# Seven half-size products in place of eight in a feed-forward down projection, its weight sums made in DRAM

## The chip, the cores and the metric

The kernel runs on one core of a Trainium2 chip. The metric is the device time of one execution in microseconds (us), lower being better. Every time below comes from one profiled execution or from the three timed runs of the kernel before.

## The reference, cut to what matters

The network has 512 tokens of width 1024 in float32. A first block (two attention-like mixers and a feed-forward block) is followed by four attention layers. The change lies in the feed-forward block of the first block:

```
h = rmsnorm(x, norm_ffn)
x = x + (silu(h @ w_ffn_gate) * (h @ w_ffn_up)) @ w_ffn_down
x = rmsnorm(x, norm_final)
```

`w_ffn_gate` and `w_ffn_up` are 1024 x 2816, `w_ffn_down` is 2816 x 1024. The hidden width 2816 is 22 chunks of 128.

## The kernel before

Matrix products are float32 products made of three terms: each operand is split into a high part (float32r, made by a copy on ScalarE, L214) and a low part (what is left, made by a subtraction on VectorE, L215), and TensorE adds high x high, low x high and high x low (`mm3`, L270 to L277). `split_into` (L213) is that pair of operations. Weights come by DMA on SyncE's queue (SP) into `wraw`, which has three buffers of 128 x 1024, and their splits go to `wpool`, which has six buffers each for high and low. `X` holds the residual, tokens by width; `Ah` and `Al` hold the normalized activations, width by tokens, already split.

`mixer1` (L425) is the first block's attention part. In `nsa` (L717) a small network compresses keys and values; its small weights `w2t` are the last DMAs (L744) that GpSimd (POOL) issues before the attention's scores. POOL's next work is the broadcast of a gain (`gf`, L858) and, block by block of 128 tokens, the two small operations of `rms_scale` (L377): a multiply-add and a power. `merge` (L850) ends the mixer; its `epilogue` (L873) adds a product to X, sums squares, calls `rms_scale`, scales, and `to_feat` (L361) transposes the block on TensorE into `Ah` and `Al`.

`ffn` (L963) works on the hidden width in three parts of 8, 8 and 6 chunks (`FF_PARTS`, L33). The first four chunks take whole gate and up products (L981 to L993) while `half_sums` (L886) makes sums of halves of the activations. All later chunks go two at a time through `pair` (L999): the gate products of two neighbouring chunks are made as seven products of half size by `halves_product` (L909), from sums of quarters of the two chunks' weights and of the activations; the two up products are whole; then come the silu, the product with up (`hidden`, L975) and the split into `hdh` and `hdl`. After the chunks of a part, `down` (L1026) multiplies them by their rows of `w_ffn_down` through `out_proj` (L397): for each half of 512 output columns and each block of 128 tokens one product over the part's chunks into a PSUM bank, then an update of X (L1029):

```
nc.vector.scalar_tensor_tensor(out=xv, in0=ps, scalar=0.5, in1=xv, op0=ALU.mult, op1=ALU.add)
```

In the last part, squares (L1033), the norm with `gf` (L1038) and `to_feat` (L1039) follow block by block, and the first products of the next layer (`mla`, L1107) read `Ah` and `Al`.

The order of instructions on each engine is worked out when the kernel is built, by a scheduler with a timing model that goes by program order where two instructions could both run; `after` (L341) adds an order by hand. Each engine then works strictly in that order. A DMA that needs another one's result waits on the engine that issues it.

Of the kernel before, what the change touches and what calls it, by code (L numbers as in the profile page):

```python
# [18 lines left out]
S = 512  # L19
# [13 lines left out]
FF_PARTS = (8, 8, 6)  # L33
# [94 lines left out]
class Net:  # L128
    def __init__(self, ctx, tc, a):
# [6 lines left out]
        self.small = pool("small", 4)  # L136
        ps = lambda name, bufs: ctx.enter_context(tc.tile_pool(name=name, bufs=bufs, space=PSUM))
# [579 lines left out]
    def nsa(self, w, gate, kp, vv, qu, spare, rope, fill_gate, fill_up, fill_last):  # L717
        nc, a, tc = self.nc, self.a, self.tc
        with ExitStack() as c1:
# [8 lines left out]
            for i, (pe, w1, w2) in enumerate((("cmp_pe_k", "cmp_k_w1", "cmp_k_w2"), ("cmp_pe_v", "cmp_v_w1", "cmp_v_w2"))):  # L728
# [14 lines left out]
                for r in range(2):  # L743
                    nc.gpsimd.dma_start(w2t[:, r], a[w2][0])  # L744
# [140 lines left out]

    def half_sums(self, pool, room):  # L886

# [3 lines left out]
        f11, f21, f12, f22 = (room.tile([128, 4, 256], F32, name=n) for n in ("f11", "f21", "f12", "f22"))  # L891
        for f, k, tok in ((f11, lo, t0), (f22, hi, t1), (f21, lo, t1), (f12, hi, t0)):
            nc.vector.tensor_tensor(out=f, in0=q(self.Ah, k, tok).bitcast(F32), in1=q(self.Al, k, tok).bitcast(F32), op=ALU.add)
        nc.vector.tensor_tensor(out=f22, in0=f21, in1=f22, op=ALU.add)
        nc.vector.tensor_tensor(out=f21, in0=f11, in1=f21, op=ALU.subtract)
        nc.vector.tensor_tensor(out=f11, in0=f22, in1=f11, op=ALU.subtract)
        nc.vector.tensor_tensor(out=f12, in0=f12, in1=f11, op=ALU.subtract)
        out = {"a11": (q(self.Ah, lo, t0), q(self.Al, lo, t0)), "a12": (q(self.Ah, hi, t0), q(self.Al, hi, t0)), "a22": (q(self.Ah, hi, t1), q(self.Al, hi, t1))}

        def splits():  # L900
            for n, src in (("s2", f11), ("s3", f21), ("s1", f22), ("s4", f12)):
                h, l = (pool.tile([128, 4, 256], F32R, name=n + u) for u in "hl")
                self.split_into(h, l, src)
                out[n] = (h, l)
            return out

        return splits

    def halves_product(self, pool, raws, sums, w, n0, out):  # L909
# [5 lines left out]
        v1 = self.wload(w, 0, KD, (n0 + 128, 128), pool=raws)  # L915
# [16 lines left out]
        def product(ps, wt, k0, name, first=False, last=False):  # L932
            sh, sl = sums[name]
            for k in range(4):
                (ah, al), (bh, bl) = (wt[0][:, k0 + k], wt[1][:, k0 + k]), (sh[:, k], sl[:, k])
                for i, (x, y) in enumerate(((ah, bh), (ah, bl), (al, bh))):
                    nc.tensor.matmul(ps, lhsT=x, rhs=y, start=first and k == 0 and i == 0, stop=last and k == 3 and i == 2, skip_group_check=True)  # L937
# [21 lines left out]
        product(a, w3, 4, "a22", last=True)  # L959
        out(0, 1, a, None)  # L960
        yield

    def ffn(self):  # L963
        nc, a, tc = self.nc, self.a, self.tc
        with ExitStack() as c1:
            f1 = c1.enter_context(tc.tile_pool(name="f1", bufs=1))
            raws = c1.enter_context(tc.tile_pool(name="fr", bufs=1))
            most = max(FF_PARTS)
            hd = [f1.tile([128, most, S], F32R, name=n) for n in ("hdh", "hdl")]
            st = f1.tile([128, NB, 2], F32, name="fss")  # L970
            gf = f1.tile([128, D], F32, name="gf")
            self.broadcast_row(gf, a["norm_final"])
            wg, wu = a["w_ffn_gate"][0], a["w_ffn_up"][0]

            def hidden(m, s, u, tok=slice(0, S)):  # L975
                nc.vector.tensor_tensor(out=s, in0=s, in1=u, op=ALU.mult)
                self.split_into(hd[0][:, m, tok], hd[1][:, m, tok], s)


            with tc.tile_pool(name="f0", bufs=1) as f0:  # L980
                for m in (0, 2):  # L981
                    wgs, wus = self.w_cols(wg, m * 128), self.w_cols(wu, m * 128)
                    for t in range(2):
                        halves = 1 if m or t else 2
                        for hf in range(halves):
# [5 lines left out]
                            s = f0.tile([128, S], F32, name="fg", bufs=2)[:, 0:n]  # L991
                            self.silu2(s, pg)
                            hidden(m + t, s, pu, tok)  # L993
# [482 lines left out]
```

## Time and profile before

| what | value |
|---|---|
| three timed runs | 1867.27, 1861.35, 1867.57 us |
| median | 1867.27 us |
| profiled execution, its own time | 1861.58 us |
| profiled execution, span from first to last instruction | 1859.8 us |
| mean granted TensorE clock | 0.998 |

The span and its parts below belong to the one profiled execution. PE is TensorE's matmuls, PEld its weight loads (which overlap matmuls), DVE is VectorE, ACT ScalarE, POOL GpSimd, SP SyncE; L12 is line 12 of the kernel. A group of instructions reads "line engine operation output<-inputs, shape, xcount | busy time, mean ns of one | idle time of the engine just before". The granted clock is a share of 2.4 GHz.

### The profile page before, as it was taken

What the parts mean: (1) busy time and instruction counts of PE and PEld (TensorE: products, weight loads), DVE (VectorE), ACT (ScalarE), POOL (GpSimd) and SP (SyncE); (2) the same over time, 40 slices, a digit from 0 to 9 for tenths busy, and PEclk for the clock granted to TensorE, in tenths of its full rate; (3) what the DMA queues carried; (4) which work ended last, traced back from release to release, by engine and by line L of the source; (5) the groups of instructions that cost most, each with busy time, mean ns of one, the idle gap of its engine ahead of it and who ended that gap; (6) DMA issues with size and microseconds to landing.
All of it is one profiled execution on the core that took longest, in us unless ns stands there. A gap on an engine that the chain in (4) does not pass through costs nothing.

```text
span 1859.8 us, 27095 instructions
## 1 busy us (share of the span) xinstructions
PE 1815.6 (98%) x10023; PEld 1492.6 (80%) x10023; DVE 1215.3 (65%) x3050; ACT 905.9 (49%) x2024; POOL 153.9 (8%) x213
## 2 busy tenths in 40 slices
PE   7999999999999999999999999999999999999997
PEld 7877787678888988889887798777888877988775
DVE  5554387754854664656878675576776666788866
ACT  4543236743432442435666434573565563366651
POOL 2211100000000000001000011341000000200001
PEclk9999999999999999999999999999999999999999
DMA  7222141042332342333121233211432222232111
GB/s 219 79 59 57 36 128 41 19 146 79 103 96 74 112 127 79 91 94 98 54 69 58 64 91 98 68 56 39 115 78 60 78 80 69 76 88 59 48 56 46
DMA packets 200751, 148.13 MB, mean 80 GB/s; under 512 B 8765, under 2 KB 178538, under 8 KB 200618
## 3 DMA queue, kind: packets, MB, share of 16 engines
q1 hardware_dynamic: 198826, 140.97, 26.4%
q0 software_dynamic: 1792, 5.42, 0.9%
q8 instruction: 79, 1.29, 0.3%
q14 instruction: 54, 0.44, 0.1%
HBM read 144.27 MB, written 2.10 MB: 79 GB/s over the span
## 4 chain that ended last, share of the span: by engine, by line
PE 91%; DVE 4%; ACT 2%; issue 2%; DMA 1%; POOL 0%; SPq 0%; POOLq 0%; DVEq 0%; ACTq 0%
PE pj L273 22%; PE pj L275 22%; PE pj L276 21%; PE o L350 4%; PE t L337 3%; PE pj L937 3%; PE s L937 1%; PE o L273 1%; PE o L276 1%; PE o L275 1%; PE s L275 1%; PE s L273 1%; PE s L276 1%; PE s L311 1%; DVE wl L215 1%
## 5 line engine op out<-in xcount | busy, mean ns | idle before, releaser
L214 ACT ACTIVATE wh<-wr 128x1024 fp32r<-128x1024 f32 (+9 forms) x406 | 294.6, 755 | 402.7 <-PE pj L275 162.5
L215 DVE TENSOR_TENSOR wl<-wr,wh 128x1024 fp32r<-128x1024 f32 (+9 forms) x406 | 337.8, 855 | 217.6 <-ACT wh L214 212.8
L273 PE MATMUL pj<-Ah,wh 128*128 128x512 f32 (+1 forms) x888 | 348.0, 392 | 2.2 <-DVE fg L288 0.9
L275 PE MATMUL pj<-Al,wh 128*128 128x512 f32 (+1 forms) x888 | 347.3, 391 | 0.2 <-DVE Al L215 0.2
L276 PE MATMUL pj<-Ah,wl 128*128 128x512 f32 (+1 forms) x888 | 346.0, 390 | 0.0
L273 PE MATMUL pj<-wh,Ah 128*128 128x512 f32 (+5 forms) x640 | 218.9, 343 | 4.4 <-ACT Ah L214 4.2
L275 PE MATMUL pj<-wl,Ah 128*128 128x512 f32 (+5 forms) x640 | 216.5, 338 | 0.0
L276 PE MATMUL pj<-wh,Al 128*128 128x512 f32 (+5 forms) x640 | 214.7, 339 | 0.9 <-DVE Al L215 0.9
L273 PEld LDWEIGHTS pj<-Ah,wh 128*128 128x128 f32 x888 | 168.1, 189 | 37.1 <-PE s L276 1.6
L276 PEld LDWEIGHTS pj<-Ah,wl 128*128 128x128 f32 x888 | 168.0, 189 | 34.7 <-issue 1.5
L275 PEld LDWEIGHTS pj<-Al,wh 128*128 128x128 f32 x888 | 168.0, 189 | 33.3 <-issue 0.8
L327 ACT ACTIVATE sp<-sp,nm 128x128 f32<-128x128 f32 (+3 forms) x256 | 142.9, 559 | 75.5 <-DVE nm L326 73.4
L205 ACT ACTIVATE pt<-t 128x512 f32<-128x512 f32 (+3 forms) x288 | 115.4, 445 | 103.7 <-PE t L337 66.7
L324 DVE CUSTOM_DVE_ANT_0 sp<-s,c_causal 128x128 f32<-128x128 f32 (+3 forms) x256 | 121.0, 486 | 56.6 <-PE s L276 23.5
L273 PEld LDWEIGHTS pj<-wh,Ah 128*128 128x128 f32 x640 | 121.3, 190 | 19.4 <-ACT Ah L214 7.0
L276 PEld LDWEIGHTS pj<-wh,Al 128*128 128x128 f32 x640 | 121.0, 189 | 12.8 <-DVE Al L215 2.0
L275 PEld LDWEIGHTS pj<-wl,Ah 128*128 128x128 f32 x640 | 121.4, 190 | 10.8 <-issue 0.2
L337 PE MATMUL t<-ident,sp 128*128 128x128 f32 x640 | 108.9, 278 | 5.1 <-ACT pt L205 4.8
L337 PEld LDWEIGHTS t<-ident,sp 128*128 128x128 f32 x640 | 77.3, 140 | 30.8 <-ACT pt L205 12.8
L331 DVE TENSOR_SCALAR sp<-sp,rc 128x128 f32<-128x128 f32 (+3 forms) x256 | 96.7, 383 | 5.0
L273 PE MATMUL pj<-wh,hdh 128*128 128x512 f32 x176 | 68.5, 390 | 0.3 <-DVE X L1029 0.3
L275 PE MATMUL pj<-wl,hdh 128*128 128x512 f32 x176 | 68.7, 390 | 0.0
(478 smaller groups left out, 3344.9 us busy)
## 6 DMA issues: line engine op xcount, KB each, us to landing
wr<-in_w_in_dram SPq DMA_DIRECT2D x34, 512.0 KB, 3.8
wr<-in_fox_w_in_dram SPq DMA_DIRECT2D x30, 512.0 KB, 4.1
wr<-in_w_ffn_gate_dram SPq DMA_DIRECT2D x22, 512.0 KB, 3.9
wr<-in_w_ffn_up_dram SPq DMA_DIRECT2D x22, 512.0 KB
wr<-in_w_ffn_down_dram SPq DMA_DIRECT2D x22, 512.0 KB, 3.9
wr<-in_swa_w_in_dram SPq DMA_DIRECT2D x20, 512.0 KB, 3.8
wr<-in_mla_w_in_dram SPq DMA_DIRECT2D x16, 512.0 KB, 4.0
wr<-in_mla_w_out_dram SPq DMA_DIRECT2D x16, 512.0 KB, 3.8
```

Of the source, the lines that this page charges most:

```text
L205: return self.nc.scalar.activation(out, in_, AF.Copy, scale=1.0 if scale is None else scale)
L214: self.nc.scalar.activation(h, src, AF.Copy)
L215: self.nc.vector.tensor_tensor(out=l, in0=src, in1=h.bitcast(F32), op=ALU.subtract)
L273: mm = self.nc.tensor.matmul(ps, lhsT=ah, rhs=bh, start=i == 0, stop=False)
L275: self.nc.tensor.matmul(ps, lhsT=ah, rhs=bl, start=False, stop=False)
L276: mm = self.nc.tensor.matmul(ps, lhsT=al, rhs=bh, start=False, stop=i == n - 1)
L324: nc.vector.tensor_tensor_reduce(out=v, in0=ps, in1=self.causal[:, S - n:S], scale=1.0, scalar=LOWEST, op0=ALU.add, op1=ALU.max, accum_out ...
L327: nc.scalar.activation(v, v, AF.Exp, bias=nm[:, g], accum_out=sm[:, g])
L331: nc.vector.tensor_scalar(v, v, rc[:, g], None, ALU.mult)
L337: nc.tensor.transpose(ps[:, (b - j) * 128:(b - j + 1) * 128], sp[:, POFF[b] + j * 128:POFF[b] + j * 128 + 128], self.ident)
L350: mm = self.nc.tensor.matmul(po[64 * i:64 * i + 64, j * 128:S], lhsT=value(j, i), rhs=pt[:, TOFF[j]:TOFF[j] + (NB - j) * 128], start=first ...
L937: nc.tensor.matmul(ps, lhsT=x, rhs=y, start=first and k == 0 and i == 0, stop=last and k == 3 and i == 2, skip_group_check=True)
```

## The change

`w_ffn_down` is taken as 2 x 2 quarters of 1408 x 512: b11, b12, b21, b22. The hidden activations are taken as 2 x 2 as well (two halves of tokens, and even against odd chunk of a pair, where a pair is now chunk c and chunk c + 11). The down product then takes seven products of half size. Four of them use sums of weight quarters, t1 = b11 + b12, t3 = b22 + b12, t2 = b22 + t1, t4 = b21 + t2, and three use b11, b22 and b21. The sums are made in DRAM, part by part, by 32 DMAs that POOL issues in `nsa` behind the small weight loads: 16 copies, and 16 transfers that add to what lies at the destination. The parts are now 3, 3, 3 and 2 pairs. The hidden activations are kept as seven split operands of 256 tokens per pair. Products of one PSUM bank run on without a fresh start, and X is updated after each of them with a sign, 14 times in a part. `gf` of the final norm is loaded in the last part, into the buffer of a gate weight. The second up product of a pair is held behind the pair's half products.

```
-FF_PARTS = (8, 8, 6)
+FF_PARTS = (3, 3, 3, 2)
...
+    def far_cols(self, w, m):
+
+        return self.w_cols(w, m * 128, 128) + self.w_cols(w, m * 128 + D_FF // 2, 128)
...
-                    nc.gpsimd.dma_start(w2t[:, r], a[w2][0])
+                    small = nc.gpsimd.dma_start(w2t[:, r], a[w2][0])
+                if i == 1:
+                    self.sum_weights(small.ins)
...
+    def sum_weights(self, last):
...
+        def dma(q, x, p, **how):
+            nonlocal last
+            d = self.nc.gpsimd.dma_start(self.down_quarter(q, p), self.down_quarter(x, p), **how).ins
+            self.after(d, last)
+            last = d
+
+        add = dict(accum_op=ALU.add, max_dma_last_dim=2048)
+        copies = lambda p: [dma(q, x, p) for q, x in (("t1", "b11"), ("t3", "b22"), ("t2", "b22"), ("t4", "b21"))]
+        copies(0)
+        for p in range(len(FF_PARTS)):
+            dma("t1", "b12", p, **add)
+            dma("t3", "b12", p, **add)
+            if p + 1 < len(FF_PARTS):
+                copies(p + 1)
+            dma("t2", "t1", p, **add)
+            if p:
+                dma("t4", "t2", p - 1, **add)
+        dma("t4", "t2", p, **add)
...
+            ops = [f1.tile([128, max(FF_PARTS), 7 * 256], F32R, name=n) for n in ("hdh", "hdl")]
...
+            def even(j, s, u):
+
                 nc.vector.tensor_tensor(out=s, in0=s, in1=u, op=ALU.mult)
-                self.split_into(hd[0][:, m, tok], hd[1][:, m, tok], s)
+                nc.vector.tensor_tensor(out=s[:, T1], in0=s[:, T0], in1=s[:, T1], op=ALU.subtract)
+                operands(j, 0, s)
+
+            def odd(j, pool, s, t, u):
+
+                nc.vector.tensor_tensor(out=t, in0=t, in1=u, op=ALU.mult)
+                e, f = (pool.tile([128, S], F32, name="fu", bufs=2) for _ in range(2))
+                nc.vector.scalar_tensor_tensor(out=e[:, T1], in0=s[:, T1], scalar=-1.0, in1=t[:, T1], op0=ALU.mult, op1=ALU.subtract)
+                nc.vector.tensor_tensor(out=e[:, T0], in0=e[:, T1], in1=s[:, T0], op=ALU.add)
+                operands(j, 4, e)
+                nc.vector.tensor_tensor(out=f[:, T0], in0=e[:, T1], in1=t[:, T0], op=ALU.add)
+                operands(j, 6, f[:, T0])
+                operands(j, 2, t)
...
+                first, _ = self.proj_feat(pu[1], wus[1], self.act)
+                self.after(first, last)
+                odd(j, f2, g[0], g[1], pu[1])
...
+                pieces = [(r, min(2, nk - r)) for r in range(0, nk, 2)]
...
+                w = load("b11")
+                pa = [self.pj(), self.pj()]
+                for i in range(2):
+                    product(pa[i], 0, w, i, first=True)
+                    update(pa[i], i, 0, 1)
+                w = load("t1")
+                pc = [self.pss(), self.pss()]
+                for i in range(2):
+                    product(pc[i], 4, w, i, first=True)
+                    update(pc[i], 2 + i, 1, 1)
...
+                w = load("b21")
+                pb = [self.pst(), self.pst()]
+                for i in range(2):
+                    product(pb[i], 2, w, i, first=True, last=True)
+                    update(pb[i], i, 0, 1)
+                    squares(i, 0)
+                    norm(i)
+                w = load("t4")
+                for i in range(2):
+                    product(pa[i], 3, w, i, last=True)
+                    update(pa[i], 2 + i, 0, 1)
+                    squares(2 + i, 0)
+                    norm(2 + i)
```

The order of the seven products is b11, t1, t2, b22, t3, b21, t4. `half_sums` makes the same sums of activations in two steps of half the rows each.

## Rows read from the trace of the kernel before

**Rows 1.** The page, busy us (share of the span) x instructions of each engine.
```profile
PE 1815.6 (98%) x10023; PEld 1492.6 (80%) x10023; DVE 1215.3 (65%) x3050; ACT 905.9 (49%) x2024; POOL 153.9 (8%) x213
```
**Rows 2.** Stretch, its length, busy us of each engine, granted clock, DMA share, GB/s.
```profile
484.00:840.00 356.00, 355.67 (x1951) 308.83 (x1951) 202.24 (x262) 130.69 (x192) 3.72 (x10) 1.00 0.32 94
...
300.00:320.00 20.00, 19.47 (x117) 13.49 (x116) 17.25 (x92) 16.36 (x50) 0.00 (x0) 1.00 0.11 33
340.00:360.00 20.00, 19.14 (x117) 13.00 (x115) 17.99 (x97) 16.45 (x52) 0.00 (x0) 1.00 0.11 27
...
476.00:484.00 8.00, 6.60 (x40) 5.96 (x39) 7.97 (x11) 1.89 (x4) 0.60 (x1) 0.80 0.60 190
...
250.00:450.00 200.00, 194.11 (x996) 148.38 (x995) 140.52 (x497) 110.14 (x266) 1.52 (x3) 1.00 0.29 86
...
240.00:260.00 20.00, 19.38 (x131) 16.55 (x130) 15.50 (x31) 8.01 (x13) 1.12 (x2) 1.00 0.54 152
```
**Rows 3.** The longest of PE's five waits, 476 to 880 us: us, times, longest.
```profile
PE pj L273 <- DVE fg L288: 0.9, 1, 0.9
```
**Rows 4.** Down matmuls: two of the timeline (start, duration), and one group.
```profile
571.04 0.39 PE L273 MATMUL pj<-wh,hdh 128*128 128x512 f32 x1
...
573.53 0.39 PE L273 MATMUL pj<-wh,hdh 128*128 128x512 f32 x1
...
L273 PE MATMUL pj<-wh,hdh 128*128 128x512 f32 x176 | 68.5, 390 | 0.3 <-DVE X L1029 0.3
```
**Rows 5.** Groups of VectorE by form, 484 to 840 us.
```profile
L215 DVE TENSOR_TENSOR wl<-wr,wh 128x1024 fp32r<-128x1024 f32 x69 | 83.3, 1222 | 50.7 <-ACT wh L214 49.9
...
L1029 DVE SCALAR_TENSOR_TENSOR X<-pj,X 128x512 f32<-128x512 f32 x24 | 16.4, 689 | 42.5 <-PE pj L276 42.2
...
L215 DVE TENSOR_TENSOR wl<-wr,wh 128x512 fp32r<-128x512 f32 x9 | 6.2, 689 | 32.2 <-ACT wh L214 32.2
...
L215 DVE TENSOR_TENSOR wl<-wr,wh 128x768 fp32r<-128x768 f32 x4 | 3.8, 954 | 1.9 <-ACT wh L214 1.9
L1008 DVE TENSOR_TENSOR fg<-part,t 128x256 f32<-128x256 f32 x9 | 3.7, 415 | 0.4 <-PE t L937 0.4
```
**Rows 6.** Groups of ScalarE by form, 484 to 840 us.
```profile
L214 ACT ACTIVATE wh<-wr 128x1024 fp32r<-128x1024 f32 x69 | 72.4, 1058 | 139.3 <-PE pj L276 59.2 <-PE pj L275 25.2 <-PE s L937 18.1
...
L214 ACT ACTIVATE wh<-wr 128x512 fp32r<-128x512 f32 x9 | 5.7, 633 | 24.9 <-PE pj L275 12.7 <-PE pj L937 11.6 <-PE pj L276 0.6
```
**Rows 7.** Timeline, the last part's norm (start, duration).
```profile
818.60 0.69 DVE L1029 SCALAR_TENSOR_TENSOR X<-pj,X 128x512 f32<-128x512 f32 x1 [2.13 <-PE pj L276]
...
821.26 1.28 DVE L1038 SCALAR_TENSOR_TENSOR X<-X,rmso,gf 128x1024 f32<-128x1024 f32 x1 [0.96 <-POOL rmso L225]
...
837.00 0.60 PE L372 MATMUL t<-ident,X 128*128 128x128 f32 x4
```
**Rows 8.** DMA queues (packets, MB, share of 16 engines); issues, KB each, us to landing.
```profile
q1 hardware_dynamic: 198826, 140.97, 26.4%
...
wr<-in_w_ffn_down_dram SPq DMA_DIRECT2D x22, 512.0 KB, 3.9
...
wr<-in_w_up_gla_dram SPq DMA_DIRECT2D x8, 256.0 KB, 3.0
...
og<-in_ln_g_dram POOLq DMA_DIRECT2D x4, 512.0 KB, 4.0
```
**Rows 9.** POOL's work around its gap (start, duration); landing of its small loads.
```profile
249.86 1.12 POOL L744 DMA_DIRECT2D w2t<-in_cmp_v_w_dram  x2 [14.98 <-PE t L760]
384.79 0.54 POOL L222 DMA_DIRECT2D gf<-in_norm_ffn_dram  x1 [133.81 <-ACT kw1h L214]
...
453.33 0.19 POOL L379 TENSOR_SCALAR rms<-ss 128x1 f32<-128x1 f32 x1 [68.00 <-DVE ss L879]
...
DMA to landing us min/median/max: 2.1/2.2/2.4
```
**Rows 10.** The longest of PE's waits, 250 to 450 us.
```profile
PE t L337 <- ACT pt L205: 1.9, 6, 0.6
```

More of the change, by code (lines that the diff above doesn't have):

```diff
@@ L890, in half_sums @@
         q = lambda t, k, tok: t[:, k, tok]
[L891 to L895, printed above, removed]
@@ L936, in product @@
                 for i, (x, y) in enumerate(((ah, bh), (ah, bl), (al, bh))):
-                    nc.tensor.matmul(ps, lhsT=x, rhs=y, start=first and k == 0 and i == 0, stop=last and k == 3 and i == 2, skip_group_check=True)
+                    mm = nc.tensor.matmul(ps, lhsT=x, rhs=y, start=first and k == 0 and i == 0, stop=last and k == 3 and i == 2, skip_group_check=True)
+            return mm.ins
         def kept(ps):
@@ L958, in halves_product @@
         out(1, 0, u2, c)
-        product(a, w3, 4, "a22", last=True)
+        end = product(a, w3, 4, "a22", last=True)
         out(0, 1, a, None)
-        yield
+        yield end
     def ffn(self):
         nc, a, tc = self.nc, self.a, self.tc
+        T0, T1 = slice(0, 256), slice(256, 512)
         with ExitStack() as c1:
@@ L980, in ffn @@
             with tc.tile_pool(name="f0", bufs=1) as f0:
-                for m in (0, 2):
-                    wgs, wus = self.w_cols(wg, m * 128), self.w_cols(wu, m * 128)
+                sums, steps = self.half_sums(f1, f0)
+                for m in range(2):
+                    wgs, wus = self.far_cols(wg, m), self.far_cols(wu, m)
+                    g = []
                     for t in range(2):
                         halves = 1 if m or t else 2
+                        s = f0.tile([128, S], F32, name="fg", bufs=2)
@@ new lines, in pair, with down, load, weights @@
+                first, _ = self.proj_feat(pu[1], wus[1], self.act)
+                self.after(first, last)
+                odd(j, f2, g[0], g[1], pu[1])
+            def down(part, nk):
+                final = part == len(FF_PARTS) - 1
+                pieces = [(r, min(2, nk - r)) for r in range(0, nk, 2)]
+                def load(q):
+                    src = self.down_quarter(q, part).rearrange("(k p) n -> p k n", p=128)
+                    out = []
+                    for r, rc in pieces:
+                        v = self.wraw.tile([128, 1024], F32, name="wr")[:, 0:rc * 512].rearrange("p (k n) -> p k n", n=512)
+                        nc.sync.dma_start(v, src[:, r:r + rc])
+                        out.append(v)
+                    return weights(out)
+                def weights(t):
+                    parts = []
+                    for v, (r, rc) in zip(t, pieces):
+                        h, l = self.wtile(rc, 512)
+                        self.split_into(h, l, v)
+                        parts.append((r, rc, h, l))
+                    return Split(parts)
+                def product(ps, q, w, i, first=False, last=False):
+                    tok = slice(q * 256 + i * 128, q * 256 + i * 128 + 128)
+                    for j in range(nk):
+                        (ah, al), (bh, bl) = (o[:, j, tok] for o in ops), w.at(j, slice(0, 512))
+                        for u, (x, y) in enumerate(((ah, bh), (ah, bl), (al, bh))):
+                            nc.tensor.matmul(ps, lhsT=x, rhs=y, start=first and j == 0 and u == 0, stop=last and j == nk - 1 and u == 2, skip_group_check=True)
+                def update(ps, b, half, sign):
+                    xv = self.X[:, b, half * 512:half * 512 + 512]
+                    nc.vector.scalar_tensor_tensor(out=xv, in0=ps, scalar=0.5 * sign, in1=xv, op0=ALU.mult, op1=ALU.add)
+                def squares(b, half):
+                    if final:
+                        sq = f2.tile([128, S], F32, name="fu", bufs=2)
+                        nc.scalar.activation(sq, self.X[:, b, half * 512:half * 512 + 512], AF.Square, accum_out=st[:, b, half:half + 1])
+                def norm(b):
+                    if final:
```

122 lines of the change are left out of this document (78 added, 44 removed).

## The prediction

> **What bounds the kernel now.** I read the page's busy times first: TensorE (PE) is busy 1815.6 of 1859.8 us, VectorE (DVE) 1215.3 [rows 1]. A busy share is a mean, so next come busy times by stretch: from 484 to 840 us, which holds nearly all of the feed-forward block, PE is busy 355.67 of 356.00 us, DVE 202.24, ScalarE (ACT) 130.69 [rows 2]. The list of PE's waits from 476 to 880 us has five entries of 0.9 us or less, 2.3 us together [rows 3]. So in this block a matmul that goes is time that goes, as long as whatever feeds PE stays ahead of it; what is taken from or added to ACT, DVE or the queues counts only where it makes PE wait.
>
> **What goes.** A matmul of the down projection starts 0.226 us after the one before (11 starts between 571.04 and 573.53 us [rows 4]; the 0.39 us that a row shows is its pipelined length). There are 528 now (three groups of 176, one of them in [rows 4]). Seven products of two token blocks, 11 chunks and 3 terms are 7 x 2 x 11 x 3 = 462. 66 x 0.2264 = **14.9 us** less on the path. Gate and up keep their matmuls: two pairs of chunks are still made in full and nine by half products.
>
> **What DVE and ACT get.** By the mean durations in [rows 5, 6], a split of an operand taken as a weight split of its width, on DVE:
> - Weight splits: 22 pieces of 1024 columns become 28 of 1024 and 21 of 512: 6 x 1.222 + 21 x 0.689 = 21.8 us.
> - Updates of X: 24 become 56: 32 x 0.689 = 22.0 us.
> - Sums of the hidden halves: four of 256 columns for each of 11 pairs, at the 0.415 us of an add of that shape: 18.3 us.
> - Splits of the operands: per pair three of 512 and one of 256 for two of 512, 0.689 + 0.415: 12.1 us.
>
> That is 74 us more: 276 of about 341, 81% where it was 57%. ACT gets at most 6 x 1.058 + 21 x 0.633 + 22 x 0.633 = 34 us, 48% in all. ACT stays covered. For DVE the trace bounds the price. At 57% PE idles 0.33 us here; in two attention stretches with DVE at 86 and 90%, PE idles 0.53 and 0.86 us in 20, at least 2.7% [rows 2]. So PE loses between 0 and 0.027 x 341 = 9 us. The high row is the nearer in load, but there each matmul needs the softmax step just before it, while weight splits run ahead in six buffers. I take **2.5 us**.
>
> **Part boundaries, now four.** Once the last up product of a part ends, its odd operand needs a product (0.69), two 256-column sums (0.83), a copy on ACT (0.63) and a split (0.69): 2.8 us. The first down product, which needs only the even operand, covers 18 x 0.2264 = 4.1 us with three pairs, 2.7 with two. One weight split of 1.22 us ahead of the chain uses up the rest. Between 0 and 4 x 1.3 us; I take **1 us**.
>
> **The last part and the norm.** This part gives PE 84 matmuls, 19.0 us. DVE has 7 x 1.222 for weights, 14 x 0.689 for updates, 3.7 for the odd operand, 4 x 0.954 for the next layer's first weights and 1.4 to the end of block 0's normalization: 27 us, of which two splits (2.4) can be done ahead. So the next layer's first matmul can come 5.7 us late. Without that load, the chain from an update to the scaled X takes 3.9 us (818.60 to 822.54), then four transposes 0.60 and a copy on ACT 0.63 [rows 6, 7]: 5 us to the first `Ah`. Block 0's last product used to have three more behind it (12 us); now one of b21 and two of t4, 6 matmuls each, leave 4.1 us, so even then PE idles about 1 us. Between 1 and 5.7; nearer the upper, as DVE works in order: **5 us**. An idle of this kind can also lower the clock: around PE's waits at the block's start the mean granted clock of 476 to 484 us was 0.80 [rows 2], a stretch at 1.2 beside one at 2.4 GHz, or 0.2 x 8 = 1.6 us of full clock. As much again at the block's end stays in the range.
>
> **Down loads on SP.** A three-pair product needs 512 and 256 KB in 4.1 us. They land in 3.9 and 3.0 us [rows 8] and are split in 2.3 and 1.3 us; through three buffers a product's weights take (6.2 + 4.3) / 3 = 3.5 us. Hidden, with 15% to spare; if loads slowed to 5 us each, it would be 4.5 us, 0.4 over, for 21 products: 8 us. The final gain's broadcast moves from the block's start to the last part, lands in 4.0 us and has five products' time, 13.6: nothing. Its POOL issue has only the two-operation norm behind it.
>
> **The 32 DMAs on POOL.** They start behind the small weight loads, about 251 us. POOL then has nothing until the gain's broadcast at 384.79 and the first norm at 453.33 [rows 9]; both are queued behind these DMAs, DVE's scaling and PE's transposes wait for the norm, and the summed weights are due later still (the first part's down matmuls run at 571 [rows 4], one pair of chunks later than they will). So they have 202 us. They issue at some 0.6 us each, 19 us. Sixteen copies move 11.5 MB. The queues moved 141 MB with 26.4% of the span, 287 GB/s [rows 8]: 40 us. Sixteen accumulations move as much again; no row shows one. An accumulation can't cost less than a copy, as it reads more: 40 us, or twice that by the bytes read, or more. Other transfers take 0.29 of these 200 us, 58 us [rows 2]. With a factor of two: 40 + 80 + 58 = 178 us, inside 202; the point from which they are late is 104 / 40 = 2.6 times a copy. The waits between them overlap, because the next part's copies are issued in between. I take **0 us**. What they do to SP's loads also has cover: PE waits for no DMA anywhere in the stretches of [rows 3, 10], whose largest wait is 1.9 us, for ACT.
>
> A POOL broadcast of 512 KB landed in 4.0 us, an SP load in 3.9 [rows 8]. The Trainium skill (DMA: Bandwidth & Descriptors, "Issuing engines are not separate DMA queues") has transfers of all issuers run on the same 16 engines, which speaks against calling the sums free; by it alone the loads would slow, as bounded above, to at most 8 us.
>
> **Sum.** -14.9 + 2.5 + 1 + 5 = -6.4 us. The profiled execution took 1861.58 us, 1859.8 of it span; it becomes 1855.2. The median of the runs is 1867.27, 5.7 above it, so the median to expect is 1861 us. About 0.5% (9.3 us) is what a measurement here can tell from no change; the forecast is 0.35%.
>
> **Rivals.**
> - *All covers hold* (0.24). The scheduler keeps DVE ahead and puts the next layer's weight splits early; only the 1 us of the unloaded chain is lost: -14.9 + 1 = -13.9, 1853 us. For it: PE's 0.33 us of idle at every pair and boundary now. Against: DVE's 27 us in a part of 19.
> - *The sums hold POOL* (0.18), the slower one. If an accumulation costs over 2.6 copies, the norm of the first block's end starts late and PE has nothing to run past 476 us. At 3 copies the lateness is 16 us, at 3.5 it is 36: -6.4 + 36 = +30, 1897 us; at 3, 1877. For it: accumulations wait in POOL's order for the DMA whose result they need. Against: the factor of two by bytes. The small POOL loads landed in 2.2 us with DVE busy 15.5 of 20 us [rows 2, 9], so DVE did not hold up their descriptors visibly. The Trainium skill (SBUF, "Who interferes with whom") says that DVE's two-port modes block GpSimd's descriptor writing; by it the attention would lengthen these 32, which is this same rival.
> - *DVE sets the pace* (0.08). At the attention's 4.3% (0.86 in 20) over 341 us PE loses 14.7, with 5.7 at the end, 8 by loads and 5 at boundaries: +18.5, 1886 us. Against: the six split buffers.
>
> **Chances and range.** The forecast has 0.50; of it 0.15 lies past -9.3 us, 0.35 within. With the first rival that is 0.39 faster. The second gives 0.16 slower and 0.02 same, the third 0.06 slower and 0.02 same: 0.39 same, 0.22 slower. By cases, no change and faster are even. The forecast's own range is 1855 to 1868. The full range goes from the first rival less the spread of the runs (1853 - 6 = 1847) to 1886, which takes in the third rival and the nearer half of the second.
>
> **What would show it.** Right: 462 down matmuls 0.226 us apart; PE idle under 4 us before the last part and some 5 at the next layer's start; DVE near 276 us in the block; POOL's DMAs over before 450 us. Wrong: the first norm's POOL operation after 453 us with PE idle behind it; PE waiting for split weights inside a part; a granted clock below 1.00 between 840 and 860 us.

## The result and the profile after

| | before | after |
|---|---|---|
| median of the runs, us | 1864.58 (1861.35 to 1867.57) | 1919.28 (1916.74 to 1921.25) |
| ratio, with its 95% interval | | 1.0304 [1.0288, 1.032] |
| profiled execution: time, span, us | 1861.58, 1859.8 | 1916.74, 1914.9 |
| mean granted clock of the span | 0.998 | 0.983 |

The changed kernel is 3% slower. The forecast was 1861 us, the range ended at 1886, and slower had 0.22. The median of before takes in the runs shown at first and those made beside the changed kernel.

First the page of the changed kernel: the engines' busy times, and POOL's DMA queue with packets, MB and share of 16 engines.

```profile
PE 1819.8 (95%) x9957; PEld 1489.1 (78%) x9957; DVE 1277.7 (67%) x3186; ACT 931.9 (49%) x2076; POOL 180.7 (9%) x245
...
q0 software_dynamic: 10752, 28.49, 6.0%
```

PE has 9957 instructions for 10023 in [rows 1]: exactly the 66 matmuls are gone. The 32 new transfers are in the queue q0. PE's share falls from 98 to 95%: of the 55.1 us that the span grew, 50.9 are time in which PE does not work. The other 4.2 are longer busy time, though there are fewer matmuls; the granted clock fell. Where the lost time lies is read from two fixed points: the first operation of the first block's norm on POOL, and the last copy of MLA's `cn` on DVE, just behind the feed-forward block. The timeline of POOL after, from the last sum to the norm:

```profile
361.66 0.87 POOL L907 DMA_DIRECT2D t<-t  x1 [6.67 <-DMA t<-t]
441.75 0.57 POOL L223 DMA_DIRECT2D gf<-in_norm_ffn_dram  x1 [79.21 <-ACT kw1h L215]
510.33 0.19 POOL L384 TENSOR_SCALAR rms<-ss 128x1 f32<-128x1 f32 x1 [68.01 <-DVE ss L886]
```

The norm comes at 510.33 us, in [rows 9] at 453.33: **57.0 us are lost before it.** POOL is not what is late. It issues its last sum at 361.66 and then sits idle for 79 us before the gain row. The second point, on DVE's timeline, before and after:

```profile
866.69 0.48 DVE L1082 TENSOR_SCALAR cn<-pj,rmso 128x256 f32<-128x256 f32 x1 [0.21 <-POOL rmso L225]
```

```profile
920.49 0.48 DVE L1231 TENSOR_SCALAR cn<-pj,rmso 128x256 f32<-128x256 f32 x1 [0.21 <-POOL rmso L226]
```

From the norm to this point it took 413.36 us before and 410.16 after. The feed-forward block, where all the arithmetic was saved, gains 3.2 us; what lies behind it takes 1.3 us more. So there are two questions: what costs 57 us in the attention, and where 11.7 of the block's 14.9 us go.

**The attention.** Stretches of the changed kernel: length, busy us of PE, PEld, DVE, ACT, POOL, granted clock, DMA share, GB/s.

```profile
260.00:280.00 20.00, 9.56 (x28) 6.85 (x28) 6.62 (x15) 1.22 (x2) 4.32 (x6) 0.71 1.06 277
280.00:300.00 20.00, 9.24 (x31) 7.47 (x32) 8.97 (x24) 4.46 (x9) 6.24 (x8) 0.61 1.09 240
300.00:320.00 20.00, 14.45 (x66) 11.15 (x64) 8.71 (x40) 5.13 (x13) 4.18 (x6) 0.83 1.07 269
...
250.00:450.00 200.00, 152.56 (x761) 111.36 (x760) 113.55 (x466) 89.96 (x237) 26.56 (x35) 0.87 0.68 165
```

For 100 us PE has half to three quarters of its work, ACT and DVE have less still, and the 16 DMA engines are busy all the time (0.11 before from 300 to 320 us, [rows 2]). All engines wait together, which points to data. The clock falls too, 0.61 in a stretch in which PE worked 9.24 us of 20. The chain of waits from 245 to 380 us (start, us, what) says for which data:

```profile
253.08 20.03 DMA wr<-in_w_in_dram
...
275.47 23.15 DMA wr<-in_w_up_gla_dram
...
300.11 31.87 DMA wr<-in_w_up_nsa_dram
...
333.44 23.25 DMA wr<-in_w_in_dram
```

Four weight loads of SP, one after the other, hold 98 us of this stretch. They are not the new transfers; they are the loads that were there before. The DMA issues from 252 to 372 us, with KB each and median us to landing:

```profile
q0 software_dynamic: 9024, 23.14, 81.6%
q1 hardware_dynamic: 12212, 6.12, 21.6%
...
t<-in_w_ffn_down_dram POOLq DMA_DIRECT2D x18, 768.0 KB, 19.2
t<-t POOLq DMA_DIRECT2D x6, 768.0 KB, 19.7
wr<-in_w_in_dram SPq DMA_DIRECT2D x8, 512.0 KB, 17.2
t<-in_w_ffn_down_dram POOLq DMA_DIRECT2D x6, 512.0 KB, 25.8
...
t<-t POOLq DMA_DIRECT2D x2, 512.0 KB, 7.7
```

A 512 KB load of SP lands after 17.2 us, where the loads of this size in [rows 8] take 3.9. POOL's transfers take 19.2 to 25.8 in the median, the last two 7.7, and are issued every 3.5 us in the mean, so five or so are under way at once (32 transfers by their median landings, some 634 us, over the 117 us from 252 to 369). How the two queues share the engines is seen from 264 to 345 us, when both had work nearly all the time (packets, MB, share):

```profile
q0 software_dynamic: 6671, 17.36, 89.3%
q1 hardware_dynamic: 6671, 3.35, 19.2%
```

They move the same number of packets (the pieces in which the engines move a transfer), 6671 each. But a packet of SP's loads here is 512 bytes, and one of POOL's is 4 KB (a copy) or 2 KB (an accumulation). So SP gets a sixth of the bytes, 3.35 MB in a stretch in which it moved 5.11 MB before. At that rate 512 KB take 12.7 us (an estimate from this row), and SP often has two loads queued. Who waits on ACT, from 250 to 450 us (us in total, times, longest):

```profile
ACT wh L215 <- DMA wr<-in_w_in_dram: 50.3, 7, 13.0
...
ACT wh L215 <- DMA wr<-in_w_up_gla_dram: 13.3, 4, 5.5
ACT wh L215 <- DMA wr<-in_w_up_nsa_dram: 7.6, 2, 5.6
```

ACT stands for 71 us (12 before) at weight splits whose raw weights have not landed, and works in order: the attention's copies and exponentials stand behind those splits. PE's own list names DVE and ACT as releasers and no DMA at all (its longest wait is 11.4 us, `pj L278 <- DVE mt L854`). The load is one step further back.

**The block.** The whole block before (first row) and after, stretches of it after, with the columns of above, and PE's two longest waits from 860 to 900 us.

```profile
453.33:866.69 413.36, 411.22 (x2294) 360.23 (x2293) 240.65 (x345) 155.73 (x258) 13.80 (x33) 1.00 0.32 94
...
510.33:920.49 410.16, 400.17 (x2228) 347.55 (x2227) 303.69 (x482) 182.77 (x310) 15.82 (x33) 1.00 0.39 115
...
540.00:870.00 330.00, 327.08 (x1790) 281.76 (x1790) 250.49 (x373) 146.55 (x220) 0.62 (x1) 1.00 0.41 122
870.00:900.00 30.00, 23.70 (x124) 20.59 (x123) 18.64 (x30) 12.79 (x30) 6.47 (x12) 0.94 0.27 78
...
890.00:895.00 5.00, 5.00 (x24) 4.97 (x24) 1.07 (x2) 1.19 (x2) 0.00 (x0) 0.72 0.00 0
```

```profile
PE t L377 <- DVE Al L216: 2.3, 1, 2.3
PE t L377 <- DVE X L1148: 2.1, 1, 2.1
```

PE idles 2.9 us in 330 up to the last part, then 6.3 in 30 around the last norm, and its clock falls for 5 us behind that idle. By the whole block, PE idles 2.1 us before and 10.0 after: 7.9 of the 11.7 us are new idle time. The other 3.8 are matmuls that took longer: PE's busy time fell by 11.05 us, for the 14.9 worked out. The fall of the clock is 1.4 of that; the rest isn't traced.

### The profile page after: what moved, and what is told of

Read it like the earlier page. It is cut to its first block, busy times and chain, and to the rows that moved or that the text cites. A ratio compares the mean times of both kernels' runs of the same rounds, so it can differ in the third digit from the quotient of the medians.

```text
span 1914.9 us, 27306 instructions
## 1 busy us (share of the span) xinstructions
PE 1819.8 (95%) x9957; PEld 1489.1 (78%) x9957; DVE 1277.7 (67%) x3186; ACT 931.9 (49%) x2076; POOL 180.7 (9%) x245
## 2 busy tenths in 40 slices
DMA packets 214368, 179.85 MB, mean 94 GB/s; under 512 B 9709, under 2 KB 179482, under 8 KB 214234
## 4 chain that ended last, share of the span: by engine, by line
PE 84%; DMA 6%; DVE 4%; ACT 3%; issue 2%; POOL 1%; POOLq 0%; SPq 0%; DVEq 0%; ACTq 0%
PE pj L278 18%; PE pj L280 18%; PE pj L281 18%; PE o L355 4%; PE t L342 3%; PE pj L1132 3%; PE pj L986 3%; DMA wr<-in_w_in_dram 3%; DMA wr<-in_w_up_nsa_dram 2%; DMA wr<-in_w_up_gla_dram 1%; PE s L1132 1%; PE s L986 1%; DVE wl L216 1%; PE s L280 1%; PE o L281 1%
## 5 line engine op out<-in xcount | busy, mean ns | idle before, releaser
L215 ACT ACTIVATE wh<-wr 128x1024 fp32r<-128x1024 f32 (+9 forms) x433 | 312.0, 753 | 440.7 <-PE pj L280 152.0
L216 DVE TENSOR_TENSOR wl<-wr,wh 128x1024 fp32r<-128x1024 f32 (+9 forms) x433 | 356.4, 848 | 239.7 <-ACT wh L215 222.0
L278 PE MATMUL pj<-Ah,wh 128*128 128x512 f32 (+1 forms) x888 | 347.6, 392 | 1.2 <-DVE k4l L216 0.8
L278 PE MATMUL pj<-wh,Ah 128*128 128x512 f32 (+5 forms) x640 | 219.0, 343 | 5.3 <-ACT Ah L215 5.1
L278 PEld LDWEIGHTS pj<-Ah,wh 128*128 128x128 f32 x888 | 167.5, 189 | 36.6 <-PE s L281 1.6
L278 PEld LDWEIGHTS pj<-wh,Ah 128*128 128x128 f32 x640 | 121.2, 190 | 20.6 <-ACT Ah L215 8.3
L215 ACT ACTIVATE Ah<-t 128x512 fp32r<-128x512 f32 x48 | 27.0, 595 | 71.0 <-PE t L377 62.2
L333 DVE RECIPROCAL rc<-sum 128x1 f32<-128x1 f32 x256 | 39.9, 159 | 29.2 <-ACT sp L332 26.7
## 6 DMA issues: line engine op xcount, KB each, us to landing
t<-in_w_ffn_down_dram POOLq DMA_DIRECT2D x18, 768.0 KB, 19.2
```

The lines of the kernel that those rows point to most:

```text
L215: self.nc.scalar.activation(h, src, AF.Copy)
L216: self.nc.vector.tensor_tensor(out=l, in0=src, in1=h.bitcast(F32), op=ALU.subtract)
L278: mm = self.nc.tensor.matmul(ps, lhsT=ah, rhs=bh, start=i == 0, stop=False)
```

## The experiments

In all of them the profiled points are the two of above: the first norm (453.33 before, 510.33 after) and the time from there to the last `cn` (413.36 and 410.16). Diffs are against the changed kernel, unless the text names another. The kernel before, run beside them, had medians of 1863.63 (first four), 1861.82 (next four) and 1862.25 us (last four).

### What in the transfers costs the 57 us

The theory was that POOL's transfers delay SP's loads. Rivals were POOL itself being held, and the new code and its order of work, which differs from the kernel before from the attention on.

**Without the sums.** The sums are not made; raw quarters of the weights are loaded in their place.

```diff
-                if i == 1:
-                    self.sum_weights(small.ins)
...
-        if q[0] == "t":
-            return self.down_sums[q][part]
+        q = {"t1": "b11", "t2": "b22", "t3": "b12", "t4": "b21"}.get(q, q)
```

> The 32 DMAs on POOL are left out, and the down products load raw quarters of the weights in place of the four sums (the same number and size of loads), so the output is another. Every engine's order up to the end of the attention is that of the kernel before. If the loss comes from the DMAs in the attention, the first norm's POOL operation is back at 453 us (510 with the change), and what is left is the feed-forward block alone: about -3 us against before (-14.9 of matmuls, some 12 of new idle time at its end and its boundaries). If the block itself lost too, the time stays above 1870 us; by the recorded sum it would be -6.

Measured: 1861.01 us, ratio 0.9983 [0.9972, 0.9994]. First norm on POOL's timeline:

```profile
454.85 0.19 POOL L384 TENSOR_SCALAR rms<-ss 128x1 f32<-128x1 f32 x1 [67.99 <-DVE ss L884]
```

55.5 of the 57 us are gone, and the block takes 410.56 us as in the changed kernel. So the loss comes from the 32 transfers, but for 1.5 us, and the products alone are worth 2.8 us, not the 6.4 of the sum.

**Copies alone.** The 16 accumulations are left out, so that the sums hold copied quarters.

```diff
         for p in range(len(FF_PARTS)):
-            dma("t1", "b12", p, **add)
-            dma("t3", "b12", p, **add)
             if p + 1 < len(FF_PARTS):
                 copies(p + 1)
-            dma("t2", "t1", p, **add)
-            if p:
-                dma("t4", "t2", p - 1, **add)
-        dma("t4", "t2", p, **add)
```

> Only the 16 copies run, the 16 accumulations are left out (the sums are not made, so the output is another). If every transfer costs by its bytes and takes the DMA engines from the weight loads, about half of the 57 us stays: some 28, the first norm near 482 us, total near 1889. If it is the accumulation that is dear, under 10 us stay (1870 or less). If it is the mere order that the scheduler chose for the attention, the loss stays whole as long as that order stays.

Measured: 1893.21 us, first norm at 485.82. Half of the transfers, with no accumulation among them, make 32 of the 57 us, so accumulating is not the matter. One stretch, 30 us long:

```profile
270.00:300.00 30.00, 8.49 (x23) 5.85 (x24) 10.13 (x22) 3.90 (x5) 2.23 (x4) 0.60 0.96 311
```

With nothing to wait for, eight copies are issued within 4.7 us, and PE then has 8.49 us of work in 30.

**A quarter of the rows.** All 32 transfers with all their waits, each over a quarter of its rows; raw quarters are loaded in place of the sums.

```diff
-            d = self.nc.gpsimd.dma_start(self.down_quarter(q, p), self.down_quarter(x, p), **how).ins
+            rows = slice(0, FF_PARTS[p] * 32)
+            src = self.down_sums[x][p] if x[0] == "t" else self.down_quarter(x, p)
+            d = self.nc.gpsimd.dma_start(self.down_sums[q][p][rows], src[rows], **how).ins
```

> All 32 DMAs with their waits and their order on POOL, but each moves a quarter of its rows, and the products load raw quarters (the output is another). PE's order in the attention is that of the kernel before. By bytes taken from the weight loads: about a quarter of 57, 14 us, first norm near 468 us, total near 1873. By a fixed price for each DMA or wait on POOL: nearly all 57 stay (1915). By the scheduler's new order alone: nothing stays (first norm at 453, total 1859).

Measured: 1867.90 us, first norm at 460.49, 7 us late; SP's 512 KB loads land in 6.6 us. A quarter of the bytes costs an eighth of the loss: neither the number of transfers nor the bytes set it in proportion.

**One at a time.** All 32 in full size, each waiting for the one before.

```diff
-            self.after(d, last)
+            self.after(d, last, mybir.DependencyClass.Sync)
```

> Each of the 32 DMAs waits for the one before it, so that one is in flight where up to five or six were. If the depth of the POOL queue is what keeps weight loads waiting, they land in under 8 us and the loss falls below 25 us (under 1885). If the engines take turns between the two queues packet by packet, one transfer in flight delays a load as much as six: loads still land in 12 us or more while one runs, the 32 take longer, and the loss stays at 40 us or more (1905 or above).

Measured: 1869.57 us. DMA issues from 252 to 372 us, then POOL's timeline to the norm:

```profile
q0 software_dynamic: 4938, 14.23, 50.4%
...
t<-in_w_ffn_down_dram POOLq DMA_DIRECT2D x16, 768.0 KB, 5.6
wr<-in_w_in_dram SPq DMA_DIRECT2D x9, 512.0 KB, 4.9
```

```profile
464.09 0.90 POOL L907 DMA_DIRECT2D t<-t  x1 [5.62 <-DMA t<-t]
465.07 0.19 POOL L384 TENSOR_SCALAR rms<-ss 128x1 f32<-128x1 f32 x1
```

SP's loads land in 4.9 us, and PE is busy 193.15 of the 200 us from 250 to 450, for 194.11 in [rows 2] and 152.56 in the changed kernel. The attention's stall is gone with every byte still moved: the sum of squares that the norm waits for is ready at 454.55, 1.5 us later than before and as late as without any sums. What is left is the norm at 465.07: the chain of 32, about 6.8 us each, ends only there, and the norm stands behind it in POOL's queue. That is the recorded rival (*the sums hold POOL*) in small. The expectation takes loads under 12 us as a sign against turns packet by packet. They are no such sign: a 768 KB transfer has 192 packets (copy) or 384 (accumulation), a 512 KB load 1024, so one transfer runs out of packets before the load does, and POOL's queue, busy half the time here (50.4%), is empty until the next.

**Short pieces.** The limit on the length of a piece is set to 128 for every transfer. The aim was pieces of 512 bytes, as in SP's loads.

```diff
-            d = self.nc.gpsimd.dma_start(self.down_quarter(q, p), self.down_quarter(x, p), **how).ins
+            d = self.nc.gpsimd.dma_start(self.down_quarter(q, p), self.down_quarter(x, p), max_dma_last_dim=128, **how).ins
...
-        add = dict(accum_op=ALU.add, max_dma_last_dim=2048)
+        add = dict(accum_op=ALU.add)
```

> The 32 transfers as in the change, with as many in flight, but each cut into pieces of 128 numbers (512 bytes) in place of 512 (2 KB), the size of the pieces in SP's own loads. Orders on PE, ACT, DVE and SP as in the changed kernel. Depth theory (what SP's loads wait for is how many of POOL's transfers are in flight): SP's loads still take 15 to 30 us, the first norm stays at 500 us or later, 1905 to 1940 us in all. Piece-length theory (a load's small pieces take turns with POOL's long ones on the 16 engines, so shorter pieces on POOL's side shorten the wait in proportion): SP's loads take 6 to 10 us, the first norm comes at 460 to 475 us, 1870 to 1885 us.

Measured: 1952.83 us, but for another reason. The packets of the whole program, then POOL's timeline at the norm:

```profile
DMA packets 298848, 179.85 MB, mean 92 GB/s; under 512 B 99821, under 2 KB 269594, under 8 KB 298714
```

```profile
538.80 2.88 POOL L907 DMA_DIRECT2D t<-t  x1 [8.31 <-issue]
...
542.33 0.19 POOL L384 TENSOR_SCALAR rms<-ss 128x1 f32<-128x1 f32 x1
```

The aim was missed. The changed kernel has 9709 packets under 512 bytes; the 90112 more are the accumulations' 11.53 MB in packets of 128 bytes, for 2 KB before, while the copies still go in packets of 4 KB. Each issue now holds POOL for 2 to 5 us, often with pauses of 6 to 10 us, the last is issued at 539 us, and the norm starts right behind it. Little more than one is under way at a time (14 issues of some 11 us in 120), SP's 512 KB loads land in 8.2 us, and PE is busy 182.47 us from 250 to 450, for 152.56 in the changed kernel. The run shows the recorded rival in full, but doesn't tell depth from piece length, since both changed and the copies kept their packets.

**Two in flight.** Each transfer waits for the last but one.

```diff
             self.after(d, last)
+            if len(chain) > 1:
+                self.after(d, chain[-2], mybir.DependencyClass.Sync)
+            chain.append(d)
             last = d
```

> The 32 transfers as in the change, each waiting for the last but one before it, so that two are in flight and never more (up to six in the changed kernel, one in the kernel with each behind the one before). Depth theory: SP's loads take 6 to 10 us, between the 4.9 us with one and the 17 to 31 us with all; PE loses 3 to 15 us before the first norm; the 32 are done by 380 to 420 us, so POOL is free in time for the gain row; first norm 456 to 468 us, 1864 to 1877 us in all. If instead any overlap among POOL's transfers has the whole price: first norm at 490 us or later, over 1895 us.

Measured: 1878.12 us, first norm at 470.15, 17 us late. One stretch, the two queues in it, and the issues from 252 to 372 us:

```profile
260.00:280.00 20.00, 14.49 (x58) 11.67 (x58) 15.68 (x41) 5.66 (x9) 3.20 (x4) 0.83 1.09 283
```

```profile
q0 software_dynamic: 1301, 3.44, 69.2%
q1 hardware_dynamic: 4401, 2.21, 39.1%
```

```profile
wr<-in_w_in_dram SPq DMA_DIRECT2D x9, 512.0 KB, 9.4
```

The engines are as busy (1.09) and move as much (283 GB/s) as in the changed kernel's row for the same stretch (1.06, 277), yet PE has 14.49 us of work there instead of 9.56. So the total bandwidth does not set the loss; the split between the queues does. With two under way POOL's queue runs empty at times, and SP moves 2.21 MB in 4401 packets, for 1301 packets of POOL's. In the changed kernel POOL's queue hardly ever empties, and in the same 20 us SP moved 0.83 MB, 1629 packets for POOL's 1628. In one line: with 0, 1, 2 and about 5 transfers under way a 512 KB load takes 3.8 (the same list of the kernel before), 4.9, 9.4 and 17.2 us, and the attention loses 0, 1 to 2, 17 and 57 us. The 17 us lie just above the 3 to 15 expected.

**At once, but beside the feed-forward block.** With the mended kernel below (only part 0 in the attention), the other 24 wait only for their data.

```diff
-            serial = True
```

> As the kernel with part 0 alone in the attention, but the 24 transfers of the second go wait for nothing but their data, as in the change, so that several are in flight beside the feed-forward block. Depth theory: SP's 512 KB loads there take 10 us or more, PE waits for weights, and the block is 15 to 60 us longer: 1865 to 1910 us. If only the attention's stretch is sensitive (its activations are behind the weight splits on ACT): under 5 us more, 1848 to 1855 us.

Measured: 1871.43 us. First norm at 453.58, but the block takes 421.03 us, 16.8 more than with the same transfers one at a time (404.25, below; the scheduler's order of work in the block differs a little too). The issues from 480 to 620 us, and the chain's two longest pieces there:

```profile
wr<-in_w_ffn_gate_dram SPq DMA_DIRECT2D x6, 512.0 KB, 14.6
wr<-in_w_ffn_up_dram SPq DMA_DIRECT2D x6, 512.0 KB, 20.4
```

```profile
530.17 17.47 DMA wr<-in_w_ffn_up_dram
547.64 23.67 DMA wr<-in_w_ffn_gate_dram
```

The stall moved with the transfers: it belongs to a queue of POOL's that hardly ever empties, not to the attention. Here SP also loads down weights and sums, in packets of 2 KB. From 515 to 521 us all packets of both queues are accumulations and loads of that length, and each queue moved 399 packets and 0.78 MB: at equal packets the bytes are shared equally.

### A version that keeps the products

**Two goes.** Parts 0 and 1 are summed in the attention, parts 2 and 3 behind the first norm's operations on POOL, always one at a time. (`last_power` is the norm's last POOL operation; `sum_weights` takes the parts to do.)

```diff
-                    self.sum_weights(small.ins)
+                    self.sum_weights(small.ins, (0, 1))
...
-            self.after(d, last)
+            self.after(d, last, mybir.DependencyClass.Sync if serial else mybir.DependencyClass.NoSync)
+            serial = True
...
+        self.sum_weights(self.last_power, (2, 3), serial=False)
         with ExitStack() as c1:
```

> The same 32 transfers, all one at a time, but in two goes: parts 0 and 1 (16 of them) in the attention from 252 us on, parts 2 and 3 (16) behind the first norm's operations on POOL, from some 480 us on, beside the feed-forward block. At 6.8 us each the first go ends at 252 + 16 x 6.8 = 361 us, ahead of the gain row, the second at some 590 us, ahead of the first load from it at some 710 us. Depth theory: no stall in either place; first norm 453 to 456 us, the feed-forward block as in the changed kernel, 1860 to 1864 us in all, that is the kernel without the sums (1861.0) again. If transfers cost by their bytes wherever they lie: the block loses 5 us or more beside the second go, 1867 us or more.

Measured: 1868.06 us (1862.78 to 1871.33), ratio 1.0038 [1.0024, 1.0052]. With the sums in two goes alone the products still bring nothing. The profiled execution, the shortest of the five, fits: norm at 453.68, block 411.77, last sum issued at 577 us. The median is 4 us above the expectation; what the longer executions lose isn't seen in this profile and stays open.

**The mended end.** Two goes, parts 2, 3, 3, 3, and b21 with the first two norms ahead of t3.

```diff
-FF_PARTS = (3, 3, 3, 2)
+FF_PARTS = (2, 3, 3, 3)
...
-                w = load("t3")
-                for i in range(2):
-                    product(pa[i], 1, w, i)
-                    update(pa[i], 2 + i, 1, -1)
-                    squares(2 + i, 1)
                 w = load("b21")
...
                     norm(i)
+                w = load("t3")
+                for i in range(2):
+                    product(pa[i], 1, w, i)
+                    update(pa[i], 2 + i, 1, -1)
+                    squares(2 + i, 1)
```

> The kernel in two goes, with two more edits for the block's end: the parts are 2, 3, 3, 3 instead of 3, 3, 3, 2, and the product with b21 (which needs only the finished operand) and the norm of the first two token blocks come before the product with t3, so that two products of nine matmul steps lie behind that norm in place of one of six. In the changed kernel PE is idle for 7.45 us of the last 40 of the block and its clock falls once. If that end is what the seven products lose, 4 to 7 us of it come back: 1855 to 1859 us. If the loss lies in the part boundaries or in DVE's share, the time stays at 1860 to 1864 us, or rises by a boundary that comes earlier.

Measured: 1850.45 us (1849.73 to 1851.95), ratio **0.994 [0.9928, 0.9953]**, faster than both kernels and below the expectation. Its whole block, the last 40 us of it in two stretches, and its `cn` on DVE:

```profile
456.74:856.03 399.29, 396.63 (x2228) 346.44 (x2227) 302.79 (x482) 183.59 (x310) 27.34 (x49) 1.00 0.54 150
...
800.00:820.00 20.00, 20.00 (x96) 16.92 (x95) 16.10 (x23) 11.07 (x18) 0.75 (x2) 1.00 0.56 166
820.00:840.00 20.00, 18.44 (x110) 16.96 (x109) 12.91 (x25) 10.46 (x31) 5.49 (x12) 1.00 0.24 76
```

```profile
856.03 0.48 DVE L1234 TENSOR_SCALAR cn<-pj,rmso 128x256 f32<-128x256 f32 x1 [0.21 <-POOL rmso L226]
```

PE idles 1.6 us in those 40 and 2.7 in the block (10.0 in the changed kernel), and the clock stays at 1.00. From the norm at 456.74 the block takes 399.29 us, **14.1 less than before**: of the 14.9 us of matmuls 14.6 are gone from PE's busy time.

**Each edit alone**, on the kernel in two goes: the parts 2, 3, 3, 3 (the first line of the diff above), and the order of the products (the rest).

> The kernel in two goes with the parts 2, 3, 3, 3 alone; the order of the products is that of the change (b21 and the first two norms behind t3). If the short last part was what uncovered the norm: 1850 to 1854 us, as with both edits (1850.5). If the order of the products was: 1858 to 1864 us.

> The kernel in two goes with the product b21 and the first two norms ahead of t3 alone; the parts stay 3, 3, 3, 2. If the short last part was what uncovered the norm: 1858 to 1864 us, as without both edits. If the order of the products was: 1850 to 1854 us. If each does half: 1854 to 1858 us in both kernels.

Measured: the parts alone 1857.59 us, 0.9976 [0.9966, 0.9985], block 409.41; the order alone 1867.30 us, 1.0034 [1.0021, 1.0047], block 416.77. None of the expected cases: neither does it alone, nor each a half. The end of the block with the parts alone:

```profile
810.00:820.00 10.00, 7.65 (x28) 5.63 (x28) 5.64 (x8) 4.25 (x7) 0.75 (x2) 0.77 0.42 127
820.00:830.00 10.00, 6.81 (x33) 5.86 (x31) 7.72 (x14) 4.43 (x11) 5.53 (x8) 0.84 0.32 98
830.00:840.00 10.00, 9.56 (x45) 9.43 (x46) 3.09 (x6) 2.37 (x5) 0.74 (x2) 0.70 0.00 0
```

PE still idles 6 us there, and the clock is down to 0.70 to 0.84 for 30 us, with 0.70 in a stretch in which PE hardly idles. Only with both edits does no wait in the block exceed 0.6 us, and then its clock is 1.00. With the order alone PE idles 13.2 us in the block; the most is for split weights, 3.7 us in three waits, 2.9 the longest; why they are late there wasn't tried.

**Part 0 alone in the attention.** The mended kernel with 8 transfers in the attention and 24 behind the norm.

```diff
-                    self.sum_weights(small.ins, (0, 1))
+                    self.sum_weights(small.ins, (0,))
...
-        self.sum_weights(self.last_power, (2, 3), serial=False)
+        self.sum_weights(self.last_power, (1, 2, 3), serial=False)
```

> The kernel of the mended end with only part 0's 8 transfers in the attention and the other 24 behind the first norm's operations, one at a time; the orders on PE, ACT, DVE and SP are the same. In the mended kernel the first norm still comes at 456.7 us against 453.3 before. If it is the 16 transfers beside the attention that cost these 3 us: first norm 453 to 455 us, and 1847 to 1850 us in all, as long as 24 x 6.8 = 163 us of transfers beside the feed-forward block cost PE nothing there. If one transfer in flight costs by its length wherever it lies: 1850 to 1853 us, the loss only moved.

Measured: 1855.70 us (1851.45 to 1858.23), ratio 0.996 [0.9948, 0.9971], above both expected cases. By the medians it is 5 us slower than the mended kernel, though the two intervals still overlap a little. The norm comes at 454.05 as expected, but the block takes 404.25 us, 5.0 more. One stretch of it:

```profile
620.00:640.00 20.00, 17.36 (x81) 14.65 (x80) 13.23 (x18) 7.67 (x9) 1.88 (x2) 0.83 0.95 205
```

With the DMA share at 0.95, PE idles 2.6 us, waiting for a weight split, and the clock falls to 0.83, worth up to 3.4 us of the 20: together enough for the 5.0. One transfer in flight is nearly free, not free.

## Why the prediction was wrong

- **The step that failed** is the 0 us of *The 32 DMAs on POOL*, in its last sentences: that SP's loads have cover because "PE waits for no DMA anywhere in the stretches of [rows 3, 10]". The runs put 55.5 of the 57.0 us on the transfers, and the trace shows the way: SP's loads got one 512-byte packet for each of POOL's of 2 or 4 KB, landed in 17.2 us instead of 3.8, and ACT stood 71 us at their splits. Two errors are in the sentence. A list of waits shows what is late now, not how much later it may become: one transfer in flight (4.9 us a load) was still covered, two (9.4 us) were not. And PE is two steps away from the loads: they hold ACT's weight splits, and ACT's order holds the attention.
- The numbers to doubt it stood in the same part. It added 178 us of transfers into 202 us, engines busy for 88% of the time, and asked only whether the transfers end in time. They did, at about 369 us. A load that comes to engines this full doesn't land in 3.9 us.
- The bound of 8 us was made for the down loads of the feed-forward block, where the change put no transfer. For the loads beside the transfers no price was worked out. That all issuers' transfers run on the same 16 engines, as the Trainium skill has it (DMA: Bandwidth & Descriptors, "Issuing engines are not separate DMA queues"), agrees with this trace: from 264 to 345 us POOL's queue fills 89.3% of the engines and SP's loads 19.2%. Read with the price of the wrong loads, it gave 8 us where the attention lost 57.
- *The sums hold POOL* was not the mechanism: POOL idles 79 us before the gain row. It is a real one, though, in the kernels with all 32 one at a time (norm at 465) and with short pieces (542).
- **What goes** was right: 66 matmuls fewer, and the mended kernel's block is 14.1 us shorter for the 14.9 worked out.
- **DVE and the part boundaries**: 2.5 + 1 us taken, 2.9 us of PE's idle measured from 540 to 870 us. DVE's load came to 76% there, for 81% forecast: from the norm to `cn` its work grew by 63 us for the 74 worked out. *DVE sets the pace* did not happen.
- **The last part** was right in kind and too small: 5 us taken, 6.3 us of idle in the block's last 30, and the fall of the clock on top, which the prediction left to the range at 1.6 us and which the trace shows (0.72 for 5 us, so 1.4 us). With the 2.9 these make 10.6 us, but not all of it is new, for PE idled 2.1 in the block before; of the 11.7 us that the block did not gain, some 2.4 stay untraced, as matmuls that took longer. Two edits, of the parts and of the order at the end, bring the block from 411.77 to 399.29 us. With them PE idles little at the end (1.6 us) and little ahead of it (0.4 from 490 to 800): the loss sat in both places.

## What to carry to other kernels

A transfer in the background is paid for by the loads that run beside it. In these traces, while it had packets waiting, the engines took one of its packets for each packet of a load, so loads in short packets beside transfers in long ones got the small part of the bytes. Price it by what a load's landing becomes at that share, and follow that landing through the engine that waits for it and whatever that engine does next in order. If such transfers are needed, let each wait for the one before and spread them over a long stretch, with nothing urgent behind them in the issuing engine's queue. When products get shorter, look at the last one before a norm first: what used to lie behind the norm as cover shrinks with them, and the clock falls with the idle.

## What the runs showed of the hardware

- The landing of a 512 KB load from SP's queue against transfers of 768 KB from POOL's under way: 3.8 us with none, 4.9 with one, 9.4 with two, 17.2 with about five. At two and five the DMA share (1.09, 1.06) and the rate (283, 277 GB/s) from 260 to 280 us were about the same; SP's part of it was 2.21 and 0.83 MB.
- While both queues had work, the engines moved as many packets of one as of the other: 6671 each from 264 to 345 us, with 3.35 MB for SP's 512-byte packets and 17.36 MB for POOL's of 2 and 4 KB; with 2 KB packets in both, 399 each and 0.78 MB each. The Trainium skill (DMA: Bandwidth & Descriptors, "Queues, rings and completion order") has each DMA engine take turns between the queues packet by packet; in the packets that the trace counts, it agrees. The number of transfers under way acts by keeping POOL's queue from running empty. No run changes the packet length of SP's loads alone.
- A copy of 768 KB from DRAM to DRAM took 5.6 us to landing with no other of them under way (median of 16 issues, four of them accumulations from the weights); an accumulation from sum to sum 6.9 (three).
- With accumulations in packets of 128 bytes instead of 2 KB, and copies still in 4 KB, an issue held POOL for 2 to 5 us instead of 0.6 to 1.0, and POOL's queue moved less than half: 10.23 MB from 252 to 372 us at 81.1% of the engines, for 23.14 MB at 81.6%.
